# Two tiles of a SwiGLU by eight plain products instead of seven combined ones, with four other edits

## The chip, the cores and the metric

The kernel runs on one core of one Trainium2 chip. The metric is device time in microseconds (us) of one execution. The engines are TensorE (PE, whose weight loads are shown as PEld), VectorE (DVE), ScalarE (ACT), GpSimd (POOL) and SyncE (SP), which issues most DMA transfers.

## The reference, cut to what matters

x is 512 rows of 1024 numbers. Two layers follow one another, and each does three steps, all in float32:

```
x = LN(ALPHA*x + 0.5*swiglu(x, ffn1_w_gate, ffn1_w_up, ffn1_w_down))
x = LN(ALPHA*x + mixer(x) @ w_out)      # retention, RG-LRU, gated delta rule
x = LN(ALPHA*x + 0.5*swiglu(x, ffn2_...) + sigmoid(x @ ple_w_gate) * (p[i] @ ple_w_proj))
swiglu(x, g, u, d) = (silu(x @ g) * (x @ u)) @ d        # d_ff = 2816
```

## The kernel before

Every large matrix product is done three times over. A float32 operand is split into a rounded part (hi) and what is left of it (lo), and hi·hi, hi·lo and lo·hi are added. ScalarE makes a hi by copying (L217, `act`). A lo is made in one of two ways: VectorE subtracts hi from the raw weights (L235, `tt`), or ScalarE copies the raw weights with a minus sign and GpSimd issues an accumulating DMA that adds them (`add_by_dma`, L429). Function `low` chooses by a flag; the first two tiles of the program use VectorE, later tiles the DMA.

Gate and up projection of a SwiGLU are 22 tiles of 128 hidden columns (`MT`). A tile is a 2 by 2 block product: x transposed is cut into four quarters A11, A12 (rows 0 to 255 of x, two halves of the depth), A21, A22 (rows 256 to 511), and the tile's weights into B11, B21 (gate) and B12, B22 (up). `Unit` does it with seven products (a Strassen-Winograd scheme) of 12 matmuls of 128x256 each (L305, `product`). Four of the seven read combinations S1 to S4 of x's quarters, made by `combine()` (VectorE sums, then hi on ScalarE and lo on VectorE, `split_quad`), and combinations T1 to T4 of the weights (steps `sum1`, `Ta`, `sum2`, `Tb` of `step_one`).

In ffn1 the first `GROUP` = 2 tiles are handled apart, because x is not complete when they begin: at the start of the program it is still being loaded, and in the second layer the norm of the layer before is still running (`pend` is the list of its threads). Both tiles first run B11 and B21, which need only A11 and A12; then the program waits for `pend`, makes the combinations, and runs T1, T2, T3, B22 and T4 for both.

Weights come in by SP's queue in raw buffers of 512 KB ([128, 1024] float32, two for each gate/up tile). There are `NRAW` of them, and `load_more` (L421) issues the next load when all readers of the buffer that stands `NRAW` back have been issued. Operands are made from them in `NSLOT` shared slots of [128, 1024].

The order of all instructions is fixed when the program is built. A planner keeps an estimated clock for each engine; the norms, the combinations, the rotary tables and the parts of the mixer are side threads (`spawn`) that are advanced while TensorE's large products are written down, and a list of `steps` says in which order weights are made ready (`prefetch` makes some ahead). Engines run their own lists in order and wait on semaphores.

At the end of each layer's mixer, `embed` computes the gate and projection of the per-layer embedding; its result sg is added to x (`tt(xt[t], xt[t], sg[t], ADD, nc.gpsimd)`, four per layer, on GpSimd). `rotary_tables` reads `positions` by DMA and makes sine and cosine tables; it begins when twelve raw buffers' loads are out.

Of the kernel before, what the change touches and what calls it, by code (L numbers as in the profile page):

```python
# [9 lines left out]
F32 = mybir.dt.float32  # L10
F32R = mybir.dt.float32r
# [11 lines left out]
GROUP = 2  # L23
NSLOT = 38
NRAW = 5
TARGET = 14.0
# [83 lines left out]
def tile_trunk(ctx: ExitStack, tc: tile.TileContext, a, out):  # L110
    nc = tc.nc
# [234 lines left out]
    plains = deque()  # L346
    COST = dict(plain=2, B11=1, B2a=2, B2b=0, sum1=1, Ta=2, sum2=1, Tb=2)
    US = 1.44
# [6 lines left out]
    def add_gu(l, w, group):  # L355
        for m in range(MT):
            j = len(loads)
            blocks4 = w[l, m].rearrange("p (g k c) -> p k g c", g=2, k=2)
            loads.append(blocks4[:, 0])
            loads.append(blocks4[:, 1])  # L360
            if m >= group:
                steps.extend((c, j, 1) for c in ("B11", "B2a", "B2b", "sum1", "Ta", "sum2", "Tb"))
            elif m == group - 1:
                js = [j - 2 * i for i in reversed(range(group))]
                dma = 1 if l else 0
                steps.extend((c, i, dma) for i in js for c in ("B11", "B2a", "B2b"))
                steps.extend((c, i, dma) for i in js for c in ("sum1", "Ta"))
                steps.extend((c, i, dma) for i in js for c in ("sum2", "Tb"))
        return j + 2 - 2 * MT
# [23 lines left out]
    for c, j, n in steps:  # L393
        if c in ("plain", "B11", "sum1", "sum2"):
            readers[j] += 1
        if c in ("B2a", "B2b", "sum1", "sum2"):
            readers[j + 1] += 1
# [52 lines left out]
    def step_one():  # L450
# [7 lines left out]
        if c == "plain":  # L458
# [5 lines left out]
            readers[j] -= 1  # L464
            o = new_op((j,), [hi, lo], [("plain", hi, lo)], 5.4)
        elif c == "B11":
            w = slots.get([128, 2, 512], F32R)
# [214 lines left out]
    def norm(t, acc, c, gb, out=None, halves_done=None, kind="whole"):  # L682
# [40 lines left out]
        names = [f"A{1 + t // 2}{q}" for q in (1, 2)]  # L723
        keep_raw, parts = kind != "whole", kind == "both" or t < 2
        while kind == "whole" and xh[0] is None:
# [37 lines left out]
    def swiglu(l, nm, pend, out=None, kind="whole"):  # L763
# [47 lines left out]
        first = gu_at[nm, l]  # L811
        ahead = (TARGET, 2, 2)
        m0 = 0
        if pend is not None:
            m0 = GROUP
            us = []
            for m in range(m0):
                us.append(Unit(m))
                for c in ("B11", "B21"):
                    us[m].run(c)  # L820
            wait(pend)
            more = combine()
            next(more)
            for c in ("T1", "T2", "T3", "B22", "T4"):
                if c in ("T2", "T3"):
                    next(more)
                for u in us:
                    u.run(c)
        last = None
# [833 lines left out]
    def embed(l, pend):  # L1663
# [12 lines left out]
        for half in range(2):  # L1676
# [34 lines left out]
            for t in tiles:  # L1711
                for h in range(2):
                    s = slice(h * 512, (h + 1) * 512)
                    stt(sg[t][:, s], sg[t][:, s], 1.0 / ALPHA, acc[t][h], MUL, MUL)
                    ps.put(acc[t][h])
                tt(xt[t], xt[t], sg[t], ADD, nc.gpsimd)
                slots.put(sg[t])
# [4 lines left out]
    def rotary_tables():  # L1722
# [5 lines left out]
        kh, kl = t_[:, 0, :], t_[:, 1, :]  # L1728
        cur[0].t += 15000.0
        yield  # L1730
# [47 lines left out]
    if True:  # L1778
# [21 lines left out]
        load_x("A12")  # L1800
        load_part(1, 0)
        load_part(2, 0)
        load_part(3, 0)
        load_x("A21")
        load_part(0, 1)
        load_part(1, 1)
        load_x("A22")
        load_part(2, 1)
        load_part(3, 1)
        nc.vector.memset(half_neg, -0.5)  # L1810
        split_quad("A11", xr["A11"])
# [101 lines left out]
```

## Time and profile before

| | |
|---|---|
| median of 3 runs | 2233.33 us (2228.46 to 2241.82) |
| the profiled execution | 2235.24 us |
| its span, first to last instruction | 2233.5 us |
| TensorE busy | 2140.7 us, 96% of the span |
| VectorE, ScalarE, GpSimd busy | 64%, 51%, 16% |
| mean granted TensorE clock | 0.974 of full speed |

The rows further down come from the profile of that execution. A row of a window gives, for a stretch of the span, each engine's busy us with its number of instructions (x), then TensorE's granted clock (1.00 is 2.4 GHz, 0.50 is 1.2 GHz), the busy share of the DMA engines and GB/s. A row of the timeline gives the start, the busy time, the engine, the line of the kernel (L305), the operation, the tile written, the tiles read and the number of like instructions in the run; in brackets stands how long the engine had been idle just before, and what released it.

### The profile page before, as it was taken

The page shows a single profiled execution, that of the slowest core. Times are in us where ns is not written, and L with a number is a line of the kernel's source. Part 1 is how long each engine was busy: PE and PEld are TensorE (multiplying, and loading weights), DVE is VectorE, ACT ScalarE, POOL GpSimd, SP SyncE. Part 2 cuts the span into 40 slices and gives each one's busy share as a digit, 9 for nine tenths or more (in the row PEclk, how much of TensorE's full clock was granted, in tenths as well). Part 3 has the DMA queues.
Part 4 walks back from the last instruction along what each step waited for, and adds up shares of the span by engine and source line. Part 5 has one row for each costly group of instructions (what it writes and reads, how often), then busy time and mean ns, then how long its engine had stood idle before and what let it go on. Part 6 is the DMA issues. An engine that isn't in the chain of part 4 may idle for free. (4 is left out here: it accounts for less than half of the span.)

```text
span 2233.5 us, 35773 instructions
## 1 busy us (share of the span) xinstructions
PE 2140.7 (96%) x14216; PEld 1921.0 (86%) x14216; DVE 1433.6 (64%) x2416; ACT 1131.4 (51%) x1899; POOL 365.2 (16%) x346
## 2 busy tenths in 40 slices
PE   6999999998899999999999999999988999999998
PEld 6899988977677899998889998888766788999987
DVE  6765636876766666664496665378776676566734
ACT  6666622646333466663266665335653345666620
POOL 1111001233221211110111110012232212111000
PEclk8999999999899999999999999999989999999999
DMA  7676632210122476664357765322002334667620
GB/s 236 164 186 167 184 105 77 94 36 11 55 68 103 104 180 165 170 167 152 94 132 179 171 166 173 106 85 67 27 10 64 114 104 102 170 163 184 194 85 38
DMA packets 105351, 270.99 MB, mean 121 GB/s; under 512 B 9440, under 2 KB 11488, under 8 KB 105184
## 3 DMA queue, kind: packets, MB, share of 16 engines
q1 hardware_dynamic: 80416, 201.07, 27.2%
q0 software_dynamic: 24768, 67.64, 16.8%
q8 instruction: 111, 1.82, 0.3%
q14 instruction: 56, 0.46, 0.1%
HBM read 198.95 MB, written 2.10 MB: 90 GB/s over the span
## 5 line engine op out<-in xcount | busy, mean ns | idle before, releaser
L305 PE MATMUL p<-s,s 128*128 128x256 f32 (+1 forms) x12000 | 1952.3, 322 | 34.6 <-ACT s L217 20.0
L305 PEld LDWEIGHTS p<-s,s 128*128 128x128 f32 x12000 | 1717.1, 192 | 194.7 <-ACT s L217 23.4
L217 ACT ACTIVATE s<-raw 128x1024 fp32r<-128x1024 f32 (+2 forms) x526 | 464.9, 909 | 232.3 <-PE p L305 154.9
L217 ACT ACTIVATE s<-s 128x256 f32<-128x256 f32 (+5 forms) x497 | 345.9, 712 | 405.7 <-PE p L305 172.8
L235 DVE TENSOR_TENSOR s<-s,s 128x1024 fp32r<-128x1024 f32 (+4 forms) x445 | 401.4, 921 | 220.8 <-ACT s L217 173.7
L217 ACT ACTIVATE s<-p 128x256 f32<-128x256 f32 (+6 forms) x740 | 282.0, 407 | 390.0 <-PE p L305 136.4
L235 DVE TENSOR_TENSOR s<-raw,s 128x512 f32<-128x512 f32 (+4 forms) x344 | 327.4, 957 | 200.2 <-issue 90.8
L429 POOL DMA_DIRECT2D s<-raw x172 | 149.0, 866 | 898.3 <-ACT s L217 728.9
L235 DVE TENSOR_TENSOR s<-p,s 128x256 f32<-128x256 f32 (+3 forms) x380 | 159.7, 432 | 90.4 <-PE p L305 64.7
L259 PE MATMUL p<-s,s 128*128 128x64 f16 (+6 forms) x1448 | 158.4, 257 | 20.4 <-DVE s L235 11.3
L235 DVE TENSOR_TENSOR s<-raw 128x512 f32<-128x512 f32 x176 | 124.7, 711 | 59.1 <-PE p L305 57.1
L669 POOL TENSOR_TENSOR rs<-rs,half_neg 128x1 f32<-128x1 f32 x24 | 34.2, 1426 | 527.2 <-DVE rs L244 527.2
L259 PEld LDWEIGHTS p<-s,s 128*128 128x128 f32 (+1 forms) x632 | 89.6, 210 | 32.7 <-DVE s L235 14.9
L239 DVE SCALAR_TENSOR_TENSOR s<-p,vecs,s 128x255 f32<-128x255 f32 (+5 forms) x128 | 69.3, 550 | 21.6 <-PE p L263 16.2
L239 DVE SCALAR_TENSOR_TENSOR x<-p,x 128x512 f32<-128x512 f32 x48 | 31.3, 682 | 72.8 <-PE p L305 72.7
L217 ACT ACT_TABLE_LOAD x50 | 64.2, 1283 | 17.6 <-DVE tails L250 8.2
L259 PEld LDWEIGHTS <-s 128*128 128x128 f16 x816 | 38.2, 101 | 24.2 <-issue 10.7
L235 DVE TENSOR_TENSOR s<-s,p 128x512 fp32r<-128x512 f32 (+2 forms) x84 | 42.8, 510 | 21.1 <-PE p L259 17.3
L263 PE MATMUL p<-cst,s 128*128 128x128 f32 x172 | 35.0, 300 | 20.6 <-DVE s L235 18.3
L235 POOL TENSOR_TENSOR s<-raw,s 128x1024 fp32r<-128x1024 f32 x14 | 35.2, 2512 | 104.8 <-ACT s L217 93.6
L235 DVE TENSOR_TENSOR s<-p,lvm 128x512 f16<-128x512 f32 x72 | 48.0, 683 | 4.9 <-PE p L259 4.7
L235 POOL TENSOR_TENSOR s<-s,cst 128x512 f32<-128x512 f32 x24 | 33.4, 1392 | 100.7 <-DVE s L235 96.0
(105 smaller groups left out, 679.9 us busy)
## 6 DMA issues: line engine op xcount, KB each, us to landing
raw<-in_wgu_dram SPq DMA_DIRECT2D x172, 512.0 KB, 4.5
raw<-in_ffn_w_down_dram SPq DMA_DIRECT2D x88, 512.0 KB, 4.0
s<-raw POOLq DMA_DIRECT2D x86, 512.0 KB, 5.1
raw<-in_win_fm_dram SPq DMA_DIRECT2D x48, 512.0 KB, 3.7
s<-raw POOLq DMA_DIRECT2D x86, 256.0 KB, 4.1
raw<-in_w_out_dram SPq DMA_DIRECT2D x16, 512.0 KB, 3.6
raw<-in_ple_w_gate_dram SPq DMA_DIRECT2D x16, 512.0 KB, 3.6
s<-in_xT_dram SPq DMA_DIRECT2D x4, 512.0 KB, 7.4
```

The costliest lines, as they stand in the source:

```text
L217: nc.scalar.activation(out=out, in_=in_, func=func, **kw)
L235: (eng or nc.vector).tensor_tensor(out=out, in0=in0, in1=in1, op=op)
L239: nc.vector.scalar_tensor_tensor(out=out, in0=in0, scalar=scalar, in1=in1, op0=op0, op1=op1)
L259: nc.tensor.matmul(out=out, lhsT=lhsT, rhs=rhs, start=start, stop=stop)
L263: nc.tensor.transpose(out, in_, idn)
L305: nc.tensor.matmul(out=out, lhsT=lhsT, rhs=rhs, start=start, stop=stop, skip_group_check=resumed)
L429: nc.gpsimd.dma_start(out=out, in_=in_, accum_op=ADD)
L669: nc.gpsimd.tensor_tensor(out=dst, in0=dst, in1=e, op=POW)
```

## The change

The two tiles at the front of each ffn1 no longer use the combinations. A new function `part(m, i, ws)` does four plain products of tile m for the upper (i = 1) or lower (i = 2) half of the rows, and both tiles have part 1, then the wait for `pend`, then part 2: eight products of 12 matmuls a tile instead of seven. `combine()`, which later tiles need, becomes a side thread beside part 2. Their weights are made by new steps P1 and P2 (hi and lo of a whole raw buffer; in halves in the first three steps of the program) in place of B11, B2a, B2b, the sums and T1 to T4. For this a norm ahead of a SwiGLU writes hi and lo quarters for all four row blocks (`parts = True`), where before it wrote them for the first two only.

The other edits: 40 slots instead of 38 and 4 raw buffers instead of 5; `embed`'s sum on VectorE instead of GpSimd; the second part of `rotary_tables`, from `yield` on, is planned 45 us behind its DMA instead of 15; at the start of the program the loads of A21 and A22 come after all weights of the two tiles.

```diff
-NSLOT = 38
-NRAW = 5
+NSLOT = 40
+NRAW = 4
...
                 dma = 1 if l else 0
-                steps.extend((c, i, dma) for i in js for c in ("B11", "B2a", "B2b"))
-                steps.extend((c, i, dma) for i in js for c in ("sum1", "Ta"))
-                steps.extend((c, i, dma) for i in js for c in ("sum2", "Tb"))
+                steps.extend((c, i, dma) for i in js for c in ("P1", "P2"))
...
+        elif c in ("P1", "P2"):
+            w = ra if c == "P1" else rb
+            hi = slots.get([128, 1024], F32R)
+            lo = slots.get([128, 1024], F32R)
+            for s in (slice(0, 512), slice(512, 1024)) if st["step"] < 3 else (slice(0, 1024),):
+                act(hi[:, s], w[:, s])
+                low(hi[:, s], lo[:, s], w[:, s], n)
...
-        keep_raw, parts = kind != "whole", kind == "both" or t < 2
+        keep_raw, parts = kind != "whole", True
...
+        def part(m, i, ws):
+
+            wait_until(lambda: len(ps.free) >= 1)
+            b = bank()
+            for c in (1, 2):
+                for k in (1, 2):
+                    key = f"B{k}{c}"
+                    if i == 1:
+                        ws[m, key] = operand((first + 2 * m, key), *ahead)
+                    hi, lo, done = ws[m, key]
+                    product(b[:, c * 256 - 256:c * 256], (hi, lo), f"A{i}{k}", k == 1)
+                    done()
+            sg = halves.get(F32)
+            s = slice(i * 256 - 256, i * 256)
+            act(sg.ap[:, 0:256], b[:, 0:256], AF.Silu)
+            tt(h[m].ap[:, s], sg.ap[:, 0:256], b[:, 256:512], MUL)
...
-            us = []
+            ws = {}
             for m in range(m0):
-                us.append(Unit(m))
-                for c in ("B11", "B21"):
-                    us[m].run(c)
+                h[m] = halves.get(F32)
+                part(m, 1, ws)
             wait(pend)
-            more = combine()
-            next(more)
-            for c in ("T1", "T2", "T3", "B22", "T4"):
-                if c in ("T2", "T3"):
-                    next(more)
-                for u in us:
-                    u.run(c)
+            if "A21" not in quad:
+                split_quad("A21", xr["A21"])
+                split_quad("A22", xr["A22"])
+            more = spawn(combine(), urgent=True)
+            for m in range(m0):
+                part(m, 2, ws)
+            wait([more])
+        free_quads("A21")
...
-                tt(xt[t], xt[t], sg[t], ADD, nc.gpsimd)
+                tt(xt[t], xt[t], sg[t], ADD)
...
-        cur[0].t += 15000.0
+        cur[0].t += 45000.0
...
+        load_part(0, 1)
+        load_part(1, 1)
         load_part(2, 0)
         load_part(3, 0)
-        load_x("A21")
-        load_part(0, 1)
-        load_part(1, 1)
-        load_x("A22")
         load_part(2, 1)
         load_part(3, 1)
+        load_x("A21")
+        load_x("A22")
```

What this does to the engines' lists is seen at three places. In the names below s is a slot, p a bank of PSUM, and a number behind a name only keeps one use apart from the next.

The first is TensorE's list at the start of the program, where the first products stand that need A21 or A22. Before, that is some 40 matmuls into the list: the end of the second tile's product over A12 (p_4, of B21; s_10 is one of A12's slots) is followed by a product of the third tile (p_5) and by the first two tiles' products over S1 (s_24):

```order
L305 MATMUL p_4_167<-s_10_121,s_16_150 128x256 x2
L305 MATMUL p_4_167<-s_10_121,s_17_151 128x256
L305 MATMUL p_5_437<-s_6_109,s_38_281 128x256 [waits DMASW0_49]
L305 MATMUL p_2_127<-s_24_209,s_20_186 128x256 [waits Activation_49]
L305 MATMUL p_4_167<-s_24_209,s_28_222 128x256 [waits DVE_49]
L305 MATMUL p_5_437<-s_6_109,s_38_281 128x256 x3
L305 MATMUL p_5_437<-s_7_110,s_38_281 128x256 x2
L305 MATMUL p_2_127<-s_24_209,s_20_186 128x256 [waits DVE_49]
L305 MATMUL p_2_127<-s_24_209,s_21_187 128x256
L305 MATMUL p_2_127<-s_24_209,s_20_186 128x256 x2
```

Now it is 96 matmuls into the list: the end of the second tile's part 1 (p_2) is followed by the first tile's part 2 over A21 (s_32, s_33):

```order
L305 MATMUL p_2_208<-s_11_124,s_17_157 128x256 x2
L305 MATMUL p_2_208<-s_11_124,s_18_158 128x256
L305 MATMUL p_2_208<-s_11_124,s_17_157 128x256 x2
L305 MATMUL p_2_208<-s_11_124,s_18_158 128x256
L305 MATMUL p_3_301<-s_32_289,s_8_115 128x256 [waits Activation_49]
L305 MATMUL p_3_301<-s_32_289,s_8_115 128x256 [waits DVE_49]
L305 MATMUL p_3_301<-s_32_289,s_9_116 128x256
L305 MATMUL p_3_301<-s_32_289,s_8_115 128x256 x2
L305 MATMUL p_3_301<-s_32_289,s_9_116 128x256
L305 MATMUL p_3_301<-s_33_290,s_8_115 128x256 [waits Activation_49]
L305 MATMUL p_3_301<-s_33_290,s_8_115 128x256 [waits DVE_49]
```

The third tile's first product (p_5), which waits for a DMA queue's semaphore (DMASW0), moved from among the first 50 matmuls to behind all 192 of the first two tiles; the only waits on x that are left in these are those for A21 and A22.

The second is TensorE's list where the second layer begins. x_82 is the last row block of x; L263 transposes it. Before, 12 matmuls stand ahead of its transposes, and S1 (s_817, s_818) right behind them:

```order
L305 MATMUL p_412_11317<-s_797_10897,s_821_11128 128x256 x6
L263 MATMUL p_410_11100<-cst,x_82 128x128 [waits DVE_49]
L263 MATMUL p_410_11100<-cst,x_82 128x128 x3
L263 MATMUL p_411_11106<-cst,x_82 128x128 x4
L305 MATMUL p_405_10993<-s_817_11115,s_794_10831 128x256 [waits Activation_49]
L305 MATMUL p_407_11040<-s_817_11115,s_803_10963 128x256
L305 MATMUL p_413_11318<-s_817_11115,s_827_11186 128x256 [waits PE_49]
L305 MATMUL p_405_10993<-s_817_11115,s_794_10831 128x256 [waits DVE_49]
L305 MATMUL p_405_10993<-s_817_11115,s_795_10832 128x256
```

Now matmuls of part 1 stand on both sides of these transposes (58 after those of the row block x_81, then 35 more), and what waits behind is part 2 over A21 (s_796):

```order
L263 MATMUL p_408_11098<-cst,x_82 128x128 [waits DVE_49]
L263 MATMUL p_408_11098<-cst,x_82 128x128 x3
L305 MATMUL p_407_11087<-s_791_10868,s_803_11028 128x256
L305 MATMUL p_407_11087<-s_791_10868,s_804_11029 128x256 [waits DMASW7_49]
L305 MATMUL p_407_11087<-s_791_10868,s_803_11028 128x256 x2
L305 MATMUL p_407_11087<-s_791_10868,s_804_11029 128x256
```

```order
L305 MATMUL p_407_11087<-s_792_10869,s_803_11028 128x256 x2
L305 MATMUL p_407_11087<-s_792_10869,s_804_11029 128x256
L305 MATMUL p_410_11188<-s_796_10972,s_784_10772 128x256 [waits Activation_49]
L305 MATMUL p_410_11188<-s_796_10972,s_784_10772 128x256 [waits DVE_49]
L305 MATMUL p_410_11188<-s_796_10972,s_785_10773 128x256
```

What moved is the first product that needs all of x: from right behind the transposes to 35 matmuls later, and it reads a quarter of x itself and no combination.

The third is VectorE's list at the end of the first layer's embedding. L239 finishes sg (s_497, s_498) out of PSUM, s_514 and s_517 are lo parts of weight combinations. Before:

```order
L239 SCALAR_TENSOR_TENSOR s_497_7398<-s_497_7398,p_344_7404 128x512 [waits PE_49]
L239 SCALAR_TENSOR_TENSOR s_497_7398<-s_497_7398,p_345_7405 128x512 [waits PE_49]
L239 SCALAR_TENSOR_TENSOR s_498_7401<-s_498_7401,p_346_7406 128x512 [waits PE_49,Activation_49]
L239 SCALAR_TENSOR_TENSOR s_498_7401<-s_498_7401,p_347_7407 128x512 [waits PE_49,Activation_49]
L235 TENSOR_TENSOR s_514_7517<-s_512_7500,s_513_7516 128x1024 [waits Activation_49]
L235 TENSOR_TENSOR s_515_7520<-raw 128x512
L235 TENSOR_TENSOR s_515_7520<-raw,s_512_7500 128x512
```

Now two of the four sums into x stand in it:

```order
L239 SCALAR_TENSOR_TENSOR s_497_7407<-s_497_7407,p_344_7413 128x512 [waits PE_49]
L239 SCALAR_TENSOR_TENSOR s_497_7407<-s_497_7407,p_345_7414 128x512 [waits PE_49]
L239 SCALAR_TENSOR_TENSOR s_498_7410<-s_498_7410,p_346_7415 128x512 [waits PE_49]
L235 TENSOR_TENSOR x_81<-x_81,s_497_7407 128x1024 [waits DVE_49]
L239 SCALAR_TENSOR_TENSOR s_498_7410<-s_498_7410,p_347_7416 128x512 [waits PE_49]
L235 TENSOR_TENSOR s_514_7529<-s_512_7508,s_513_7528 128x1024 [waits Activation_49]
L235 TENSOR_TENSOR x_82<-x_82,s_498_7410 128x1024 [waits DVE_49]
```

The sums of x moved from GpSimd's list into VectorE's, and one of them stands ahead of a lo (s_514) and one behind it.

## Rows read from the trace of the kernel before

**Rows 1.** Waits of TensorE over the whole span: us in total, times, longest us.
```profile
PE p L263 <- DVE s L235: 21.8, 12, 2.8
PE p L305 <- ACT s L217: 20.0, 11, 6.7
```

**Rows 2.** Windows at the start of the program.
```profile
0.00:100.00 100.00, 75.88 (x538) 72.75 (x539) 74.23 (x127) 64.16 (x101) 13.25 (x21) 0.88 0.75 206
17.00:34.00 17.00, 9.81 (x43) 9.01 (x43) 9.52 (x12) 9.34 (x16) 3.37 (x5) 0.50 0.80 244
100.00:120.00 20.00, 20.00 (x166) 19.79 (x165) 13.04 (x20) 13.32 (x25) 3.48 (x4) 1.00 0.68 162
```

**Rows 3.** Timeline, first 85 us.
```profile
6.72 3.23 PE L305 MATMUL p<-s,s 128*128 128x256 f32 x12 [6.72 <-ACT s L217]
...
9.77 0.63 ACT L217 ACTIVATE s<-raw 128x512 fp32r<-128x512 f32 x1 [0.16 <-DMA raw<-in_wgu_dram]
...
19.52 2.93 PE L305 MATMUL p<-s,s 128*128 128x256 f32 x12 [1.45 <-ACT s L217]
...
28.19 9.90 PE L305 MATMUL p<-s,s 128*128 128x256 f32 x58 [5.74 <-DMA s<-raw]
...
77.15 0.43 DVE L250 CAST s<-s 128x512 f32<-128x512 int32 x1 [5.37 <-DMA s<-in_positions_dram]
...
80.17 5.06 PE L305 MATMUL p<-s,s 128*128 128x256 f32 x22 [5.47 <-DVE s L235]
```

**Rows 4.** Window of the first loads.
```profile
10.00:24.00 14.00, 7.58 (x38) 6.38 (x38) 10.77 (x14) 9.79 (x14) 2.50 (x4) 0.75 0.99 342
```

**Rows 5.** Windows where the second layer begins.
```profile
1120.00:1140.00 20.00, 17.11 (x114) 15.12 (x112) 18.48 (x30) 13.61 (x25) 4.08 (x4) 1.00 0.53 145
1140.00:1160.00 20.00, 17.38 (x128) 17.09 (x129) 18.80 (x27) 13.48 (x25) 1.75 (x2) 0.83 0.33 80
```

**Rows 6.** Timeline where the second layer begins.
```profile
1128.93 1.28 DVE L239 SCALAR_TENSOR_TENSOR x<-p,x 128x512 f32<-128x512 f32 x2
...
1137.67 1.09 PE L263 MATMUL p<-cst,x 128*128 128x128 f32 x8 [1.41 <-DVE x L239]
...
1141.42 1.01 PE L305 MATMUL p<-s,s 128*128 128x256 f32 x3 [2.66 <-ACT s L217]
...
1143.63 4.60 PE L305 MATMUL p<-s,s 128*128 128x256 f32 x25 [1.20 <-DVE s L235]
```

**Rows 7.** Timeline at the end of the first layer's embedding.
```profile
775.69 5.81 POOL L235 TENSOR_TENSOR x<-x,s 128x1024 f32<-128x1024 f32 x2
776.76 2.48 DVE L235 TENSOR_TENSOR s<-s,s 128x1024 fp32r<-128x1024 f32 x1
...
779.16 2.89 DVE L235 TENSOR_TENSOR s<-raw 128x512 f32<-128x512 f32 x1
...
784.13 6.09 PE L305 MATMUL p<-s,s 128*128 128x256 f32 x34 [2.70 <-ACT s L217]
```

**Rows 8.** VectorE's instructions by line and shape: busy us, mean ns, idle before.
```profile
L235 DVE TENSOR_TENSOR s<-s,s 128x1024 fp32r<-128x1024 f32 x178 | 219.9, 1237 | 152.7 <-ACT s L217 106.8 <-PE p L305 45.3
...
L235 DVE TENSOR_TENSOR s<-raw 128x512 f32<-128x512 f32 x176 | 124.7, 711 | 59.1 <-PE p L305 57.1 <-DMA raw<-in_wgu_dram 1.5
```

**Rows 9.** Large products (L305) alone, in the middle of the first layer's mixer.
```profile
545.00:575.00 30.00, 0.08 (x1) 0.08 (x1) 0.66 0.00 1
```

**Rows 10.** Timeline, raw buffers in a steady stretch of gate and up tiles.
```profile
204.11 1.14 ACT L217 ACTIVATE s<-raw 128x512 fp32r<-128x512 f32 x2
...
209.10 0.86 POOL L429 DMA_DIRECT2D s<-raw  x1 [2.70 <-DVE s L235]
```

**Rows 11.** DMA issues: KB each, median us from issue to landing.
```profile
raw<-in_wgu_dram SPq DMA_DIRECT2D x172, 512.0 KB, 4.5
...
s<-raw POOLq DMA_DIRECT2D x86, 512.0 KB, 5.1
```

More of the change, by code (lines that the diff above doesn't have):

```diff
@@ L346, in tile_trunk @@
     plains = deque()
-    COST = dict(plain=2, B11=1, B2a=2, B2b=0, sum1=1, Ta=2, sum2=1, Tb=2)
+    COST = dict(plain=2, P1=2, P2=2, B11=1, B2a=2, B2b=0, sum1=1, Ta=2, sum2=1, Tb=2)
     US = 1.44
@@ L393, in tile_trunk @@
     for c, j, n in steps:
-        if c in ("plain", "B11", "sum1", "sum2"):
+        if c in ("plain", "P1", "B11", "sum1", "sum2"):
             readers[j] += 1
-        if c in ("B2a", "B2b", "sum1", "sum2"):
+        if c in ("P2", "B2a", "B2b", "sum1", "sum2"):
             readers[j + 1] += 1
@@ L465, in step_one @@
             o = new_op((j,), [hi, lo], [("plain", hi, lo)], 5.4)
+        elif c in ("P1", "P2"):
[5 more added lines that the diff above has]
+                low(hi[:, s], lo[:, s], w[:, s], n)
+            readers[j + int(c == "P2")] -= 1
+            o = new_op((j,), [hi, lo], [(nm, hi[:, s], lo[:, s]) for nm, s in (("B%s1" % c[1], slice(0, 512)), ("B%s2" % c[1], slice(512, 1024)))], 2 * US)
+            o.uses = 4
         elif c == "B11":
@@ L812, in swiglu @@
         ahead = (TARGET, 2, 2)
+        def part(m, i, ws):
[13 more added lines that the diff above has]
+            tt(h[m].ap[:, s], sg.ap[:, 0:256], b[:, 256:512], MUL)
+            sg.put()
+            ps.put(b)
         m0 = 0
```

## The prediction

> **What bounds the kernel now.** TensorE is busy 96% of the span, so time can only come from where it idles, runs at its lower clock, or does fewer matmuls. I read its waits first, then the windows and timelines of the stretches where they lie. The reader is to see in the list of waits [rows 1] that they are few and of two kinds: transposes that wait for VectorE, 21.8 us in 12 waits, and large products that wait for ScalarE's copies, 20.0 us in 11. By stretches, the first kind lies in the two mixers, which the change does not rewrite; the second lies at the start, where the second layer begins, and at the end of the two embeddings: the places that the change touches.
>
> **The start, before.** In a steady stretch 166 matmuls of 128x256 take 20.00 us, 0.1205 us each. In the first 100 us only 538 run [rows 2], which is 64.8 us of work: 35.2 us are lost. The timeline [rows 3] shows where: the first product begins at 6.72 and takes 3.23 us for 12 matmuls; at 28.19 TensorE has waited 5.74 us for an accumulating DMA (the third tile's lo, whose product stands early in the list); at 80.17 it has waited 5.47 us for a VectorE that itself sat 5.37 us on the transfer of the positions at 77.15. Between 17 and 34 us the granted clock is 0.50, the lower level, and only 43 matmuls run [rows 2].
>
> **The start, after.** The eight products are 24 matmuls more for the two tiles together: 24 x 0.1205 = 2.9 us. In return nothing but quarters of x themselves is needed for 192 matmuls, and the DMA wait stands behind them. When can these run? The first 12 run as before. The next product needs A12 and B21, whose copy begins at 9.77 today [rows 3], with the same transfers ahead of it. ScalarE's list now has the tile's first raw buffer's other half ahead of it: 9.77 + 0.63 + 0.63 (two copies) + 0.7 (the lo, by the 711 ns of a 128x512 [rows 8]) = 11.7 us. The 180 matmuls left take 21.7 us at the full rate and end at 33.4; all 192 would take 23.1, so 10.3 us are lost. A21 and A22, now last in the loads, bind no one by this estimate: the DMA engines move 342 GB/s here [rows 4], at which the 4 MB of the start are 12.3 us; with the first few us of issuing they have landed about 16 us in, and two copies and two subtractions a quarter make them ready near 20; part 2 begins at 11.7 + 84 x 0.1205 = 21.8. That cover is under 2 us, so it is a risk.
>
> What follows is not in the trace. Copies of banks and of the third tile's weights queue on ScalarE, and S1 to S4 must be ready on VectorE when the third tile comes: I take 3.0 us, between 0 and 6 (one more stall like the 5.74). For the clock I take 2.2 us: it has fallen at about 17 us after a sparse start, and came back at 34 after 6 us of unbroken matmuls from 28.19. If it falls again ahead of the run, 6 us at half rate cost 3; bounds 0 and 6. The wait for the positions goes, since the table's second part is planned 30 us later and the transfer is then long done; it is inside the 35.2. Gain: 35.2 - 2.9 - 10.3 - 3.0 - 2.2 = **16.8 us**, bounds 10 and 22.
>
> On the clock the Trainium skill ("TensorE: Matmul & The Clock Gate", Part 1) says that the throttled state is the default and that activity releases it. The row agrees, at 0.50 in the sparse stretch; taken at its word, with a start of single products and gaps up to 11.7, the first eight products would run at the lower level and the gain would be some 6 us less. That is the first rival below.
>
> **The second layer's beginning.** The two windows [rows 5] hold 2.9 us of idle time, and 128 matmuls where 166 fit: 20 - 15.4 = 4.6 us more. In all 7.5 us, of which the timeline [rows 6] names 1.41 (x's last row block), 2.66 and 1.20 (S1 on ScalarE and VectorE), and the rest the lower clock (0.83 in the second window). After: from the sum into x at 1128.93 to its transposes at 1137.67 the chain takes 8.7 us. 58 matmuls of part 1 (7.0 us) now stand ahead of these transposes, so 1.7 us of waiting are left; 35 more (4.2 us) cover the copies behind them, and the combinations are made beside part 2. The clock then need not fall. 24 more matmuls cost 2.9: 7.5 - 1.7 - 2.9 = **3 us** gained, bounds -3 (the stall comes back through the accumulating DMAs, which these weights wait for in this layer) and 5.
>
> **The embedding's sum.** GpSimd's two sums beginning at 775.69 take 5.81 us [rows 7]. Beside them two VectorE instructions take 2.48 and 2.89 us that take 1.24 and 0.71 on the mean [rows 8]: 3.4 us lost on VectorE, ahead of the lo and copy that TensorE waits 2.70 us for at 784.13. On VectorE the same two sums are 2 x 1.24 = 2.5 us, by the s<-s,s row of the same shape. So VectorE is about 0.9 us earlier; 1 us a layer with what the clock gives back, **2 us** in all. Bounds: +9, if the waits with their slow clock vanish in both layers; -5, if the sums simply stand in front of the late lo.
>
> A rule speaks against this edit. The Trainium skill ("Perfetto Trace Analysis", Optimizing Scalar/DVE Operations) has work moved from a saturated VectorE to GpSimd, with the doubt that the shared port may spoil it. VectorE is not saturated here as a whole, and the doubt is what the long rows show; by the rule alone the sums would cost 5 us over both layers, by the rows they give 2.
>
> **Slots and raw buffers.** A ring of four buffers gives less time. In a gate/up stretch a tile (two buffers) takes 84 x 0.1205 = 10.1 us, so a buffer comes round in 20.2 us with four, 25.3 with five. One tile's buffers are read from 204.11 to 209.96 [rows 10], the accumulating DMA reads on for 5.1, and the load took 4.5 [rows 11]: 4.5 + 5.85 + 5.1 = 15.5 us, under 20.2. Price nothing; cover 4.7 us. The two slots more allow the planner a little more run-ahead: nothing, too. In the mixers the order is planned anew from these numbers: the change is of unknown sign, and I take 0, between -8 and +8 (a third of the 21.8 us).
>
> **Sum.** 16.8 + 3 + 2 = 21.8 us. The profiled execution took 2235.24 us, so 2213.4; the median of the runs shown lies 1.9 lower, so **2212 us**.
>
> **Rivals.**
> *The start stays cold or waits for A21.* The clock falls again and part 2 finds its quarter late. For it speaks the 0.50 of rows 2 and the thin cover of 2 us; against it, that from 11.7 on nothing in the list has to wait. Price: 3 us of clock more and 4 of waiting, so 2219 us.
> *The gain is given back later.* VectorE and ScalarE now make S1 to S4 beside part 2 and the third tile comes at once; if VectorE is late there, the wait moves to the third tile. For it speaks that S1 alone was waited for 2.66 and 1.20 us [rows 6]; against it, that part 2 gives them 96 x 0.1205 = 11.6 us of cover. A wait of 6 us in each layer (four combinations' worth of the above would be more), with the clock falling behind it (2 us), leaves 21.8 - 16 = 6: 2228 us, no change that can be told.
> *Four raw buffers starve the weights: slower.* Place: the 84 gate/up tiles that remain plain units. For it: the cover fell from 9.7 to 4.7 us. If the buffer's round is longer than the 15.5 above by more than 4.7, each tile waits; at 0.39 us a tile, 33 us, the gain is used up and 11 us (0.5%) beyond it are lost. At that point 2245 us; I price it at 2250. Against it: with five buffers no row of ScalarE's waits names these loads in the steady stretch from 120 to 300 us.
> *The mixers come out better*, by the 8 us above: 2204 us. While they run there is a stretch of 30 us without any large product [rows 9], so a change of their order can show at all.
>
> **How the numbers follow.** Chances: the forecast 0.50 (2207 to 2217), the cold start 0.17, given back 0.15, starved 0.08, better mixers 0.10. I leave out of the range the starved case and the upper half of "given back", and the far end of the better mixers: 2201 to 2227. A difference under 0.5% (11.2 us) is about what measurement can't tell from no change: under 2222.2 is faster, over 2244.5 slower. Forecast, cold start and better mixers are faster but for a small share, and a small part of "given back" is too: 0.76; same 0.16; slower 0.08.
>
> **What would show it.** In the changed kernel's profile: 192 matmuls in an almost unbroken run from about 12 to 35 us; no 5.7 us wait for an accumulating DMA at 28 and none for the positions near 77; some 700 matmuls in the first 100 us; at the second layer's beginning one wait of 1 to 2 us ahead of x's last transposes and none for S1; at the embedding's end no VectorE row of 128x1024 over 2 us. Wrong would make it: a clock of 0.50 through part 1 and part 2, a wait of several us at A21 or at the third tile, ScalarE waiting for raw buffers in steady gate/up tiles, or longer waits of transposes in the mixers.

## The result, and the profile after

The changed kernel takes 2170.09 us (median of 4 runs, 2168.70 to 2170.71) against 2234.07 for the kernel before: a ratio of 0.971, with a 95% interval of 0.968 to 0.974. That is 64 us, three times the 22 that were forecast and outside the range. The profiled execution has a span of 2166.9 us and a mean clock of 0.989.

To see where the time came from, I cut the span at the six places in which the last large product of a step is added to x (L239, `x<-p,x`, eight instructions each time). The rows of tile x give their number, their duration (shortest, median, longest, in ns), and the start of the first and of the last. The kernel before:

```profile
L239 DVE SCALAR_TENSOR_TENSOR x<-p,x x8: 673/680/692, 357.6 to 383.6; 128x512 f32<-128x512 f32 x8
...
L239 DVE SCALAR_TENSOR_TENSOR x<-p,x x8: 674/680/692, 694.2 to 721.6; 128x512 f32<-128x512 f32 x8
...
L239 DVE SCALAR_TENSOR_TENSOR x<-p,x x8: 673/680/692, 1102.5 to 1129.5; 128x512 f32<-128x512 f32 x8
...
L239 DVE SCALAR_TENSOR_TENSOR x<-p,x x8: 672/680/692, 1459.7 to 1485.7; 128x512 f32<-128x512 f32 x8
...
L239 DVE SCALAR_TENSOR_TENSOR x<-p,x x8: 672/680/691, 1794.5 to 1822.4; 128x512 f32<-128x512 f32 x8
...
L239 DVE SCALAR_TENSOR_TENSOR x<-p,x x8: 672/681/691, 2202.3 to 2225.6; 128x512 f32<-128x512 f32 x8
```

The changed kernel:

```profile
L239 DVE SCALAR_TENSOR_TENSOR x<-p,x x8: 675/681/692, 344.1 to 369.7; 128x512 f32<-128x512 f32 x8
...
L239 DVE SCALAR_TENSOR_TENSOR x<-p,x x8: 674/681/692, 657.2 to 683.8; 128x512 f32<-128x512 f32 x8
...
L239 DVE SCALAR_TENSOR_TENSOR x<-p,x x8: 675/682/692, 1060.8 to 1088.0; 128x512 f32<-128x512 f32 x8
...
L239 DVE SCALAR_TENSOR_TENSOR x<-p,x x8: 673/681/694, 1419.2 to 1445.3; 128x512 f32<-128x512 f32 x8
...
L239 DVE SCALAR_TENSOR_TENSOR x<-p,x x8: 674/681/692, 1732.6 to 1759.3; 128x512 f32<-128x512 f32 x8
...
L239 DVE SCALAR_TENSOR_TENSOR x<-p,x x8: 674/682/692, 2135.7 to 2159.1; 128x512 f32<-128x512 f32 x8
```

The differences of the last starts are the lengths of the steps (the start of the program up to the first):

| step | before | changed | gained | forecast |
|---|---|---|---|---|
| first ffn1, with the start | 383.6 | 369.7 | 13.9 | 16.8 |
| first mixer | 338.0 | 314.1 | 23.9 | 0 |
| first embedding and ffn2 | 407.9 | 404.2 | 3.7 | 1 |
| second ffn1 | 356.2 | 357.3 | -1.1 | 3 |
| second mixer | 336.7 | 314.0 | 22.7 | 0 |
| second embedding and ffn2 | 403.2 | 399.8 | 3.4 | 1 |

The places that the forecast spoke of gave 19.9 us together, in place of 21.8. The other 46.6 us come from the two mixers, whose code the change does not touch.

TensorE's waits in the changed kernel (us in total, times, longest us) answer to [rows 1]. The transposes' waits for VectorE, 21.8 us before, are down to 2.8, although no edit rewrites the code of the mixers, in which they lay:

```profile
PE p L259 <- DVE s L235: 10.5, 10, 1.7
PE p L305 <- ACT s L217: 7.6, 2, 7.5
PE p L305 <- DVE s L235: 6.7, 2, 6.4
...
PE p L263 <- DVE x L239: 4.3, 1, 4.3
PE p L263 <- DVE s L235: 2.8, 8, 0.6
```

The windows of the start answer to [rows 2]:

```profile
0.00:100.00 100.00, 86.04 (x667) 83.98 (x668) 74.94 (x131) 69.59 (x112) 23.55 (x25) 0.97 0.81 228
0.00:40.00 40.00, 32.48 (x243) 31.47 (x244) 29.65 (x43) 32.16 (x51) 14.00 (x14) 1.00 0.96 298
40.00:100.00 60.00, 53.56 (x426) 52.51 (x426) 45.29 (x88) 37.43 (x63) 9.55 (x11) 0.94 0.71 181
```

667 matmuls run in the first 100 us, where 538 did, and 243 of them in the first 40, in a row that gives a clock of 1.00. For the first few microseconds that figure does not hold. TensorE alone, in two windows of the run's beginning and in one behind it:

```profile
8.00:12.00 4.00, 3.94 (x16) 1.00 1.05 399
14.00:18.00 4.00, 4.00 (x36) 1.00 1.06 377
43.86:50.69 6.83, 3.21 (x15) 0.50 0.60 178
```

From 8 to 12 us TensorE has no gap to speak of and still runs 16 matmuls, where from 14 to 18 us it runs 36: the first products run at about half pace, as at the lower of the two clocks, though the rows give 1.00 for both stretches. Once the matmuls have stopped at 41 us, the clock falls to 0.50, from 43.9 to 50.7.

The timeline shows what is left there, against [rows 3]:

```profile
7.46 33.59 PE L305 MATMUL p<-s,s 128*128 128x256 f32 x250 [7.46 <-ACT s L217]
...
44.93 0.43 DVE L250 CAST s<-s 128x512 f32<-128x512 int32 x1 [6.14 <-DMA s<-in_positions_dram]
...
47.48 37.73 PE L305 MATMUL p<-s,s 128*128 128x256 f32 x295 [6.44 <-DVE s L235]
```

One run of 250 matmuls goes from 7.46 to 41 us. Then TensorE still waits 6.44 us behind the conversion of the positions: the wait has only moved from 77 to 45 us.

### The profile page after: what moved, and what is told of

Same layout as the page of the kernel before. It is cut to its first block, busy times and chain, and to the rows that moved or that the text cites. A ratio compares the mean times of both kernels' runs of the same rounds, so it can differ in the third digit from the quotient of the medians.

```text
span 2166.9 us, 35741 instructions
## 1 busy us (share of the span) xinstructions
PE 2119.7 (98%) x14264; PEld 1907.6 (88%) x14264; DVE 1411.5 (65%) x2408; ACT 1118.9 (52%) x1887; POOL 348.7 (16%) x332
## 5 line engine op out<-in xcount | busy, mean ns | idle before, releaser
L305 PE MATMUL p<-s,s 128*128 128x256 f32 (+1 forms) x12048 | 1949.0, 321 | 14.4 <-ACT s L217 7.6
L305 PEld LDWEIGHTS p<-s,s 128*128 128x128 f32 x12048 | 1713.6, 191 | 170.8 <-DVE s L235 13.6
L217 ACT ACTIVATE s<-s 128x1024 fp32r<-128x1024 f32 (+5 forms) x485 | 336.9, 710 | 338.0 <-DVE s L235 179.3
L235 DVE TENSOR_TENSOR s<-s,s 128x1024 fp32r<-128x1024 f32 (+4 forms) x433 | 384.5, 910 | 178.7 <-ACT s L217 138.5
L235 DVE TENSOR_TENSOR s<-raw,s 128x1024 fp32r<-128x1024 f32 (+2 forms) x344 | 327.7, 957 | 226.5 <-ACT s L217 191.5
L217 ACT ACTIVATE s<-p 128x256 f32<-128x256 f32 (+5 forms) x740 | 279.3, 407 | 300.0 <-PE p L305 120.4
L235 DVE TENSOR_TENSOR s<-p,s 128x256 f32<-128x256 f32 (+4 forms) x376 | 156.9, 433 | 76.3 <-PE p L305 48.3
L259 PE MATMUL p<-s,s 128*128 128x128 f16 (+6 forms) x1496 | 154.4, 250 | 8.3 <-DVE s L235 7.2
L235 DVE TENSOR_TENSOR s<-raw 128x512 f32<-128x512 f32 x168 | 115.1, 687 | 68.7 <-PE p L305 63.5
L677 POOL TENSOR_TENSOR rs<-rs,half_neg 128x1 f32<-128x1 f32 x24 | 35.3, 1473 | 509.6 <-DVE rs L244 509.6
L259 PEld LDWEIGHTS p<-s,s 128*128 128x128 f32 (+1 forms) x680 | 91.1, 197 | 22.0 <-issue 6.0
L239 DVE SCALAR_TENSOR_TENSOR s<-p,vecs,s 128x255 f32<-128x255 f32 (+5 forms) x128 | 69.5, 551 | 21.1 <-PE p L263 16.1
L239 DVE SCALAR_TENSOR_TENSOR x<-p,x 128x512 f32<-128x512 f32 x48 | 31.5, 683 | 49.7 <-PE p L305 49.5
L259 PEld LDWEIGHTS <-s 128*128 128x128 f16 x816 | 36.9, 100 | 21.6 <-issue 11.5
L235 DVE TENSOR_TENSOR s<-s,p 128x512 fp32r<-128x512 f32 (+3 forms) x92 | 45.8, 503 | 14.1 <-PE p L259 12.3
L263 PE MATMUL p<-cst,s 128*128 128x128 f32 x172 | 32.5, 287 | 8.6 <-ACT s L217 5.3
L239 DVE SCALAR_TENSOR_TENSOR x<-x,rs,s 128x1024 f32<-128x1024 f32 (+1 forms) x25 | 30.9, 1240 | 11.0 <-POOL rs L677 11.0
```

The source lines that it names most:

```text
L217: nc.scalar.activation(out=out, in_=in_, func=func, **kw)
L235: (eng or nc.vector).tensor_tensor(out=out, in0=in0, in1=in1, op=op)
L239: nc.vector.scalar_tensor_tensor(out=out, in0=in0, scalar=scalar, in1=in1, op0=op0, op1=op1)
L259: nc.tensor.matmul(out=out, lhsT=lhsT, rhs=rhs, start=start, stop=stop)
L263: nc.tensor.transpose(out, in_, idn)
L305: nc.tensor.matmul(out=out, lhsT=lhsT, rhs=rhs, start=start, stop=stop, skip_group_check=resumed)
```

## The experiments

Lengths of steps in what follows are differences of the same last starts, read in each kernel's own trace. Times are medians; the ratios are to the runs of the kernel before on the same chip. A length comes from one profiled execution and is less exact than it looks. The kernel before and two experiments that change nothing in the first ffn1 have 383.6, 380.6 and 382.3 us there; the changed kernel and two such experiments 369.7, 371.4 and 372.2. So a difference of up to 3 us in one step shows nothing by itself, and the start's gain is 11.1 us in the mean of these, where the two profiles above gave 13.9.

**The two numbers alone, and all but these.** Slots and raw buffers are changed together, as the change does it. The edit of the first, to the kernel before (the second is its reverse, in the changed kernel):

```diff
-NSLOT = 38
-NRAW = 5
+NSLOT = 40
+NRAW = 4
```

> The kernel before with 40 slots and four raw buffers and nothing else of the change. Theory A: the mixers' part of the gain (46.6 us by the times at which x gets its sums) comes from the slots, since the planner then lets the mixer's threads begin earlier. Then each mixer takes about 314 us from x's last ffn1 sum to its last mixer sum, the start keeps its losses, and the time is about 2187 us (2234 less 47). Rival B: the mixers gain from the other edits (norms that write quarters, the eight products' shift). Then each mixer stays at about 337 us and the time at about 2234.

> The changed kernel with 38 slots and five raw buffers again. Theory A: the mixers go back to about 337 us each, the time is about 2217 us (2170 and 47), which is 17 to 20 faster than before by the start and the embeddings. Rival B: mixers at about 314 us, time about 2170.

Measured: the two numbers alone 2194.68 us, ratio 0.982 (0.980 to 0.984), with mixers of 313.8 and 312.9 us and a first ffn1 of 383.6, as before. All but these 2207.95 us, ratio 0.988 (0.986 to 0.990), with mixers of 340.1 and 335.8, a first ffn1 of 368.5 and a second of 351.3. So the mixers' gain comes from the two numbers, and the rest of the change gives 29 us without them, more than the 17 to 20 expected. That it is the slots, for the larger part at least, is seen further down: the kernel with 39 slots has five raw buffers as well, so it differs from this one by a single slot, and its mixers are shorter by 17.0 and 14.9 us. The two gains, 42 and 29, sum to 71 against 2236.63 in these runs; the whole change gave 64. Some of what is missing lies in the second ffn1, which takes 351.3 us with five raw buffers and 357.3 with four.

What this does in a mixer is seen by comparing the kernel before with the first experiment, since both reach the mixer at 383.6 us. The first fence is of the kernel before, the second of the experiment; each row gives, for the large products alone (L305), TensorE's busy time and their number, then the granted clock, the DMA engines' share and GB/s:

```profile
504.00:544.00 40.00, 16.48 (x41) 1.00 0.05 14
544.00:584.00 40.00, 5.15 (x17) 0.74 0.00 1
584.00:624.00 40.00, 21.88 (x79) 1.00 0.23 77
```

```profile
504.00:544.00 40.00, 11.58 (x29) 1.00 0.00 1
544.00:584.00 40.00, 23.41 (x86) 0.96 0.17 54
584.00:624.00 40.00, 28.24 (x101) 0.96 0.26 82
```

From 544 to 584 us the kernel before runs 17 large products at a mean clock of 0.74, the experiment 86 at 0.96. The large products are the work that can fill TensorE while the mixer's small steps wait for one another; they were missing in the stretch to which [rows 9] belong. Of the small steps, two tiles tell the order: id is read by the transposes in the delta rule's inner solution (four for each of three head pairs and two halves), and sstate by its recurrence. Kernel before, then the experiment:

```profile
L263 PE MATMUL p<-id,s x24: 218/219/314, 455.2 to 553.2; 128*128 128x128 f16 x24
...
L259 PE MATMUL p<-sstate,s x36: 270/275/522, 523.6 to 664.3; 128*128 128x128 f32 x36
```

```profile
L263 PE MATMUL p<-id,s x24: 218/219/231, 453.0 to 512.5; 128*128 128x128 f16 x24
...
L259 PE MATMUL p<-sstate,s x36: 270/275/418, 524.2 to 640.2; 128*128 128x128 f32 x36
```

By windows of 10 us the first five groups of transposes stand in the same windows in both, between 450 and 510; the sixth stands at 553.2 us before and at 512.5 with 40 slots. The recurrence, which needs it, ends 24 us earlier, and so does the mixer. Slots can act through the planned order, since a thread of the mixer goes on only when some number of them is free; the next two kernels change the order and leave the memory as it is.

**One threshold.** The edit, to the kernel before, and its counterpart in the changed kernel:

```diff
-ROOM_D = 4
+ROOM_D = 3      # kernel before; 6 in the changed kernel
```

> The kernel before (38 slots, five raw buffers) with one number changed: the threads that make the decay factors of the delta rule (decays) begin a head pair at three free slots, not four (ROOM_D). Theory A, sharper: this is the threshold that two more slots lift, so this alone gives a good part of the mixers' gain: about 2200 to 2215 us. Rival C: it is another threshold, or the sum of several: 2230 to 2240.

> The changed kernel (40 slots, four raw buffers) with the same threshold at six free slots, which undoes for this thread alone what the two slots give. Theory A, sharper: the mixers go back to near 337 us each and the time to about 2210 to 2217. Rival C: the mixers stay near 314, the time near 2170 to 2180.

Measured: 2210.18 us, ratio 0.989 (0.986 to 0.991), mixers 328.6 and 324.2, for the lower threshold with 38 slots; 2193.34 us, ratio 0.981 (0.979 to 0.983), mixers 325.6 and 326.7, for the higher one with 40. Each moves about half of the mixers' difference, in the direction that theory A said, so the order of the threads is a cause by itself, with the memory unchanged. The step that I named was wrong, though: the decay factors' matmuls of the kernel before run from 405.9 to 485.7 us, those of the lower threshold from 403.2 to 487.5, no earlier. What moves in the first of the two is again the sixth group of transposes:

```profile
L263 PE MATMUL p<-id,s x24: 217/219/230, 449.8 to 515.7; 128*128 128x128 f16 x24
...
L259 PE MATMUL p<-sstate,s x36: 270/275/421, 521.4 to 653.9; 128*128 128x128 f32 x36
```

It stands at 515.7 us, which is 135 us after this mixer's beginning at 380.6, against 170 in the kernel before and 129 with 40 slots. But the recurrence ends only 7 us earlier than before by the same count, not 24. In the changed kernel with the higher threshold the sixth group does not move at all:

```profile
L263 PE MATMUL p<-id,s x24: 218/219/232, 443.2 to 499.8; 128*128 128x128 f16 x24
...
L259 PE MATMUL p<-sstate,s x36: 270/275/422, 512.7 to 639.6; 128*128 128x128 f32 x36
```

It stands 128 us behind the mixer's beginning at 371.4, as early as with 40 slots, and yet the recurrence ends at 268 us by this count, against 256 in the changed kernel and 281 before. With 39 slots it is the same, 127 and 266. So an early sixth group goes with about half of the mixers' gain and does not bring the other half, which is lost or won in the recurrence behind it. What decides there was not taken apart.

**39 slots.**

> The changed kernel with 39 slots and five raw buffers (the same memory). The planned order of the mixers is then a third one. Theory F: with five raw buffers the second ffn1 takes about 351 to 352 us, as with 38 and five. Theory A: the mixers take neither 314 nor 338 but what the third order gives, between the two if free slots as such decide; a time over 338 or under 314 would say that the order's details decide. Time 2175 to 2205.

Measured: 2177.10 us, ratio 0.975 (0.973 to 0.978); mixers 323.1 and 320.9, second ffn1 351.5. In between, as free slots would have it; and the second ffn1 has its 6 us back, with five raw buffers and the eight products.

**Fewer slots asked for still.** In the kernel with both repairs (below):

```diff
-GUARD = 6
-ROOM_1, ROOM_2, ROOM_3, ROOM_O, ROOM_R = 5, 4, 3, 2, 5
+GUARD = 5
+ROOM_1, ROOM_2, ROOM_3, ROOM_O, ROOM_R = 4, 3, 2, 1, 4
```

> The kernel with both repairs and the thresholds on free slots in the mixer lowered by one (as one slot more would), of which only that ahead of the delta rule's third step changes the planned order, by about a tenth of it. If more room always helps, the mixers fall below 312 us each, time about 2155 to 2160. If the order's details decide: 312 to 320, time 2163 to 2175.

Measured: 2169.17 us, ratio 0.969 (0.965 to 0.973). The profiled execution has mixers of 321.8 and 320.9 us, 7 us more each than without this edit. Its four runs spread from 2153.96 to 2175.71, more than any other kernel's here, and the profile is of the slowest. In its first mixer TensorE is idle for 11 us, against 10 without the edit; the 7 us are matmuls that took longer, 311.0 us for 304.0, at a mean clock of 0.95 for 0.97. The fastest run is faster than any of the kernel without the edit. Whether lower thresholds help or the order's details decide stays open.

**The embedding's sum alone.** In the kernel before:

```diff
-                tt(xt[t], xt[t], sg[t], ADD, nc.gpsimd)
+                tt(xt[t], xt[t], sg[t], ADD)
```

> The kernel before with the embedding's sum on VectorE and nothing else. Theory E: this alone makes the 3.5 us a layer from x's mixer sum to its second ffn sum (407.9 to about 404.3, 403.2 to about 399.7), about 2228 against 2235. Rival: those microseconds come with the order of the weights' steps that the other edits shift; then 407 and 403 stay.

Measured: 2229.18 us against 2233.83, ratio 0.997 (0.996 to 0.999). Embedding and ffn2 take 403.7 and 398.9 us, 4.2 and 4.3 less than before: this edit alone makes that part. The whole kernel gained 4.7 us, with an interval of about 3 to 9, so that the 8.5 of the two steps are near its upper end. In the changed kernel the end of the embedding answers to [rows 7]:

```profile
727.83 24.41 PE L305 MATMUL p<-s,s 128*128 128x512 f32 x162
...
739.01 1.22 DVE L235 TENSOR_TENSOR x<-x,s 128x1024 f32<-128x1024 f32 x1
...
740.75 1.22 DVE L235 TENSOR_TENSOR s<-s,s 128x1024 fp32r<-128x1024 f32 x1
...
741.88 1.23 DVE L235 TENSOR_TENSOR x<-x,s 128x1024 f32<-128x1024 f32 x1
```

A sum takes 1.22 us on VectorE, the lo beside it (740.75) 1.22 and not 2.48, and TensorE runs through from 727.83 to 752.2 without the wait of 2.70 us. The lower clock behind that wait (0.72 from 784 to 790 us before) is gone with it.

**The positions.** In the changed kernel, the loads of x's four row blocks are taken out of `consts` and issued later:

```diff
                 spawn(rotary_tables())
+            if st["loaded"] == 24:
+                x_rows()
```

> The changed kernel with the loads of x's four row blocks (2 MB) put behind the transfer of the positions on SP's queue. Theory D: the wait of 6.4 us that TensorE still has at 47 us in the changed kernel is a VectorE that sits 6.1 us on that transfer, as at 77 us before; then it goes, and with the copy that waits behind it the first SwiGLU's last sum into x comes 5 to 8 us earlier than 369.7, the time is about 2163 to 2165. Rival: VectorE is late there anyway (S1 to S4 and the third tile's weights), the wait stays by 4 us or more, and the time is 2168 to 2170.

Measured: 2166.96 us, ratio 0.970 (0.968 to 0.972); the first ffn1's last sum at 366.0, 3.7 us earlier, where 5 to 8 were expected. Two later kernels with this edit have 364.4 and 366.1; the mean of the three is 5.6 us under that of the three without it. The timeline:

```profile
29.73 20.05 PE L305 MATMUL p<-s,s 128*128 128x256 f32 x155
...
38.40 0.42 DVE L250 CAST s<-s 128x512 f32<-128x512 int32 x1
```

The conversion begins at 38.40 without a wait, one instruction ahead of the place in VectorE's list where it sat 6.14 us on the transfer. TensorE's 6.44 us are gone from that place, and the first 100 us hold 705 matmuls in place of 667; the clock does not fall behind it. Waits of 0.60 and 1.27 us come up behind it, near 50 and 53 us.

**The second layer's beginning.** In the changed kernel this shows, against [rows 6]:

```profile
1092.49 1.06 ACT L217 ACTIVATE s<-raw 128x1024 fp32r<-128x1024 f32 x1 [5.26 <-DMA raw<-in_wgu_dram]
...
1095.75 0.86 POOL L427 DMA_DIRECT2D s<-raw  x1 [7.92 <-ACT s L217]
1096.31 0.88 POOL L677 TENSOR_TENSOR rs<-rs,half_neg 128x1 f32<-128x1 f32 x1
1097.23 1.28 DVE L239 SCALAR_TENSOR_TENSOR x<-x,rs,s 128x1024 f32<-128x1024 f32 x1 [4.75 <-POOL rs L677]
...
1098.57 1.11 PE L263 MATMUL p<-cst,x 128*128 128x128 f32 x4 [4.35 <-DVE x L239]
```

With four raw buffers ScalarE waits 5.26 us for a load. Behind it stands the copy whose accumulating DMA GpSimd is to issue, behind that in GpSimd's list the norm's rs (L677), behind that x on VectorE, and TensorE's transposes wait 4.35 us. The edit takes the accumulating DMA out of this chain:

```diff
-                dma = 1 if l else 0
+                dma = 0
```

> The changed kernel in which the first two tiles of the second layer too get their lo parts from VectorE, and no accumulating DMA. Theory F: at the second layer's beginning the norm's rs stands behind an accumulating DMA on GpSimd, this behind a copy on ScalarE that waited 5.3 us for a load with four raw buffers, and TensorE so waits 4.3 us for x; with no such DMA in GpSimd's list the wait falls under 1.5 us, and the second ffn1 takes about 352 us, not 357.3: time about 2165. Rival: VectorE, with eight subtractions more, is late instead, and 357 or more stay: 2170 to 2175.

Measured: 2166.51 us, ratio 0.970 (0.967 to 0.973); second ffn1 354.8 us. Two later kernels with this edit have 354.1 and 354.2, four without it and with four raw buffers 356.4 to 357.6: some 2.7 us, about half of what was expected.

```profile
1090.95 1.48 POOL L677 TENSOR_TENSOR rs<-rs,half_neg 128x1 f32<-128x1 f32 x1 [2.30 <-DVE rs L244]
...
1092.51 1.28 DVE L239 SCALAR_TENSOR_TENSOR x<-x,rs,s 128x1024 f32<-128x1024 f32 x1
...
1097.95 1.03 PE L263 MATMUL p<-cst,x 128*128 128x128 f32 x8
```

GpSimd's rs now follows VectorE at 1090.95, x is ready by 1093.8, and the transposes at 1097.95 wait for nothing. ScalarE's own wait for a load is still 4.7 us here, and 354.8 is not the 351.5 of five raw buffers. With five, in the kernel with all but the two numbers, no wait of ScalarE's there names a load.

**The old order of loads at the start.** In the changed kernel, A21 behind the first halves of the weights and A22 ahead of the last.

> The changed kernel with the old order of loads at the start (A21 after the first halves, A22 ahead of the last halves). If the new order carries part of the start's gain, the first product with B12 or B21 of the second tile waits for its weights, and the first SwiGLU's last sum comes 2 to 5 us after 369.7; by my working (A21 and A22 bind no one, weights come first) I expect about 2 us, time about 2172. If the order of loads does not matter: 369.7 within 1 us.

Measured: 2169.73 us, ratio 0.970 (0.969 to 0.972); the first ffn1's last sum at 371.6, 1.9 us later in the profiled execution; neither this nor the time tells it from the changed kernel. The trace does not say that the order is without effect, though. In the first 40 us 216 matmuls run, not 243. ScalarE sits 7.26 us, up to 37.0, on a transfer of constants that was issued at 28.54 behind loads of weights and of x's quarters on the same queue, and TensorE waits 7.89 us for it at 44.41. The wait of 6.44 us behind the positions is gone in return. In both orders one small transfer is late behind large ones; the order chose which.

**Without the eight products.** The kernel before with 40 slots, four raw buffers, the embedding's sum on VectorE and the later tables.

> Everything of the change but the eight products, with their weights' steps, quarters from the norm and load order: the kernel before with 40 slots, four raw buffers, the embedding's sum on VectorE and the later second part of the tables. If the parts add, the first ffn1 stays at about 383, the mixers are at 314, the embeddings at 404 and 399, and the time is about 2186 (2194.7 less 8); the eight products are then worth about 16 us at the start and less than 3 at the second layer. Rival: the later tables carry the start, ffn1 falls to 375 or less, time 2178.

Measured: 2184.37 us, ratio 0.977 (0.975 to 0.979); first ffn1 381.0, mixers 314.3 and 313.6, embeddings and ffn2 402.5 and 399.8, second ffn1 359.2. The parts add: with four raw buffers the eight products, with what belongs to them, are worth 11.3 us at the start, not the 16 expected, and 1.9 in the second ffn1, which is under what one profile can show. The first ffn1's 381.0 lies among the lengths of the kernel before, so no gain of the later tables is shown.

**Both repairs.** The two edits above (x's rows later, lo by VectorE) in the changed kernel.

> The changed kernel with both repairs: x's rows loaded behind the positions, and the second layer's first two tiles with lo parts by VectorE. Theory: the two act in different places and add, 3.7 and 2.5 us by the times of x's sums: about 2163 us, against about 2170 for the changed kernel. Rival: the order of one spoils the other, 2167 or more.

Measured: 2159.41 us (5 runs, 2158.34 to 2165.53), ratio 0.967 (0.965 to 0.968) to the kernel before. First ffn1 364.4, second 354.1; the first 100 us hold 713 matmuls at a clock of 1.00. The gain on the changed kernel is more than the 6.2 us expected: all five runs are under the lowest of the changed kernel, 2168.70, and under the lowest of the old load order on the same chip, 2167.18.

## Why the prediction was wrong

**The step that failed** is the one on slots and raw buffers: "In the mixers the order is planned anew from these numbers: the change is of unknown sign, and I take 0, between -8 and +8 (a third of the 21.8 us)", with "the two slots more ... nothing, too" ahead of it. It measured 46.6 us in the changed kernel and 48.0 with the two numbers alone. The sign I could not read from the trace. The bound could have been read: it was a third of the waits that bear one label, and a mixer loses more than that. TensorE in the first mixer: its window before, its window with the two numbers alone, and the two waits that cost most before:

```profile
384.00:722.00 338.00, 312.06 (x2076) 0.95 0.18 60
```

```profile
384.00:698.00 314.00, 302.87 (x2078) 0.98 0.21 65
```

```profile
PE p L263 <- DVE s L235: 11.4, 6, 2.8
PE p L259 <- DVE s L235: 7.7, 7, 3.2
```

Before, TensorE is idle for 26 us of 338. The label that was used has 11.4 of these; the others, of L259 above all, bring the listed waits to 25.3. Beside the idle time, the slow clock (0.74 in the 40 us from 544) stretches the matmuls that do run. With the two numbers changed the same work takes 303 us busy and 11 idle: of the 24 us gained 15 are idle time, and 9 are matmuls that took less time. [Rows 9], 30 us with next to no large product, were in hand, and were used to say that a change could show, not how large it could be. The rival "the mixers come out better" had the right sign, at 0.10 and 8 us. That more slots give an order with less of both is shown; why, only in part, by the sixth group of transposes.

That the places which the forecast named gave 19.9 us for 21.8 is luck: against the forecast the start is 2.9 us short, the second ffn1 4.1 short, and the embeddings 5.1 over.

**The start** was right in mechanism and short in size: 13.9 us for 16.8, or 11.1 in the mean of three profiles each. The forecast had 192 matmuls done at about 33 us; with 243 done at 40 us that is what ran. No late A21 came, and the wait for an accumulating DMA at 28 us is gone. What failed is the sentence that the wait for the positions goes. The transfer was issued at 29.95 us behind 2 MB of x on the same queue, and VectorE came to the conversion at 38.8, where before it did at 71.8; putting x behind the transfer gave 3.7 us in one profile, 5.6 in the mean of three, by which the term comes out at 16.7. The cold start came, but briefly: half pace up to 13 us, of which the forecast had counted all but the last microsecond or so as a slow start anyway. The rule weighed there, of the Trainium skill ("TensorE: Matmul & The Clock Gate", Part 1), has the throttled state as the default; the trace agrees, with 16 matmuls in the 4 us from 8 and 36 in the 4 us from 14. The price set on it, eight products at the lower level, did not come. It was also summed wrongly: 96 x 0.1205 is 11.6 us more at half pace, not 6.

**The second layer's beginning** was forecast at +3 us and came out at -1.1 in the changed kernel. The products did their part: with five raw buffers the second ffn1 took 351.3 us against 356.2, a gain of 4.9. The forecast's rival, that four raw buffers starve the weights, took place here, 5.26 us on ScalarE, and passed through GpSimd's list to x; repairing that path gave back about half of the 6 us. In the steady tiles it did not take place: no wait of ScalarE's from 120 to 300 us names these loads in the changed kernel either, and embedding and ffn2 take 404.2 and 399.8 us with four, 403.8 and 399.7 with five. The cover of 4.7 us that I worked out held there. In the forecast the 2.9 us of idle time belong to the first of the two windows alone; the second's 2.6 are inside its 4.6, so that the sum of 7.5 stands.

**The embedding's sum** was mis-sized: 2 us forecast, 7.1 measured in the changed kernel and 8.5 alone, near the upper bound of 9 that was given. The reading of the long VectorE rows was right. What failed is taking the gain from VectorE's 0.9 us: TensorE's whole wait of 2.70 us went, and with it the lower clock behind it, some 1.7 us more (6 us at 0.72). Why all of the wait went was not taken apart. The rule of the Trainium skill ("Perfetto Trace Analysis", Optimizing Scalar/DVE Operations) that weighed against the edit, to move work from a saturated VectorE to GpSimd, comes with a doubt about the port that the two share. The trace agrees with the doubt: VectorE's sum took 2.48 us beside GpSimd's and 1.22 without.

## What to carry to other kernels

In a kernel whose order is planned from numbers such as a count of buffers, a change of one number is a change of the order in every stage that asks for it: its possible price is all that the stage loses now, idle time and slow clock together, and not the waits under one label. Two builds that differ in that number alone tell it apart at once. Steps of one profile can be compared only beyond what kernels with the same list differ by, here 3 us. Where a wait is removed by delaying its reader, look whether the reader's place in its engine's list moved, and what stands ahead of the transfer on its queue.

## What the runs showed of the hardware

The positions' transfer, 128 rows of 512 numbers, took 15 us from its issue at 29.95 to the conversion at 44.93 with 2 MB of x ahead of it on the queue; near 72 us in the kernel before, without them, it took 5; with x behind it, it was there 9.7 us after its issue at the latest. An addition of 128x1024 into x takes 1.22 us on VectorE and 2.67 on GpSimd in the mean of eight, and while GpSimd's ran, VectorE's own of that size took 2.48. At the start of the program TensorE ran 16 matmuls in 4 us and soon after 36, with a granted clock of 1.00 in both rows: there the pace has to be read, not the clock.
